# Diff attention: where ScalarE and VectorE do a head's normalisation among the next head's work

## The chip, the cores and the metric

The kernel runs on one core of one Trainium2 chip. The metric is the device time of one execution in microseconds (us); lower is better. The core has five engines that run their own instruction queues in order: TensorE (PE: matrix products and transpositions, written to PSUM banks), VectorE (DVE), ScalarE (ACT), GpSimd (POOL) and SyncE (SP, which here only issues transfers).

## The reference

One decoder layer on 512 tokens of width 1024, in float32. Two attention branches run side by side on the same normalised input; the change lies in the second one, differential attention with four heads:

```python
scores = jnp.einsum('bqhmd,bshmd->bhmqs', qblk, k) * scale      # two maps m per head
scores = scores - slopes[:, None, None, None] * delta           # causal, ALiBi
p = jax.nn.softmax(scores, axis=-1)
a = p[:, :, 0] - lam * p[:, :, 1]
out = jnp.einsum('bhqs,bshe->bqhe', a, v)                       # 128 values per head
...
out = _rmsnorm(out, subln_g) * (1.0 - lam_init)                 # per head and token
...
merged = (sigmoid(ga) * (out_a @ w_branch_swa) + sigmoid(gd) * (out_d @ w_branch_diff))
x = x + gate1 * (merged @ w_out)
```

A gated MLP with a causal convolution and a final RMSNorm follow.

## The kernel before, in words

Every float32 product is done as three products of a high and a low part: `split` makes them, a cast on ScalarE for the high part and a subtraction on VectorE for the low part. TensorE's queue is in an order written out by hand (`manual_schedule`); VectorE, ScalarE and GpSimd are ordered in this stretch by a scheduler that takes what is ready, by priority. `tc.high_priority(offset=HP)` puts a block ahead of other ready work, and `tc.issue_after(x)` keeps what is traced in the block behind instruction `x` on that engine's queue. Every engine then runs its queue strictly in this order, so an instruction that waits holds up all that stand behind it.

TensorE fills the time between the steps of attention with "fillers": each call of `fill(1)` runs one step (three products of 512 columns) of a projection from the list `units`. `after(n, fn)` runs `fn` after n more fillers.

Differential attention goes over 16 blocks, s = 4h + n for head h (0 to 3) and token block n (0 to 3). For each block TensorE makes the scores (`sd`), VectorE adds the distance term and takes the maximum, ScalarE the exponentials, VectorE the difference of the two maps, TensorE turns the result (`td`), and ScalarE and VectorE store it as high and low part (`aTh`, `aTl`). When a head has its four blocks, `diff_values(h)` does:

- TensorE: the products with the values, `od`, in the PSUM bank of tag `v`, of which there is one (`vbank`, bufs=1).
- ScalarE: the square `sq` and the scaled copy `of` of `od`.
- `STAT_LAG[h]` = 6 fillers later, `stats`: TensorE sums the squares (`pss`, the same bank of tag `v`), VectorE makes `ms` from them, GpSimd the inverse root, into four columns of `cols`.
- `ROW_LAG[h]` fillers after that, `to_rows`: TensorE turns the columns (`rs`, again tag `v`), ScalarE copies the piece, GpSimd writes it to DRAM (`rs0d` to `rs3d`) and reads it back as a row on all partitions (`rb`).
- `NORM_LAG[h]` fillers after `stats`, `spread`: VectorE multiplies `of` by `rb`, and `split` writes the high and low part into `vvh` and `vvl`, over the head's values. The product waits in the queue behind the last two weight splits (`recent`).

`of` has two buffers, taken in turn (tags `kvA`, `kvB`); `rb` of heads 0 to 2 has one. `vvh` and `vvl` are read only by the products `pB`, after all heads. Around this stretch VectorE also does modulation rows (`ra`, from `ada_rows`), and both engines split the weights of gates and branches (`wga`, `wba`, `wgd`, `wbd`), which load through four raw buffers that VectorE frees; `ta` and `tdall` are the gates' values.

Of the kernel before, what the change touches and what calls it, by code (L numbers as in the profile page):

```python
# [10 lines left out]
AF = mybir.ActivationFunctionType  # L11
ALU = mybir.AluOpType
# [15 lines left out]
HP = 100000  # L28
# [3 lines left out]
G1_AT = 12  # L32
M5_AT = 4
STAT_LAG = (6, 6, 6, 6)
ROW_LAG = (8, 8, 8, 5)
NORM_LAG = (34, 34, 34, 24)
VA_AT = 5
SWA_FILL = (2, 1, 6, 2, 2, 2, 2, 5, 0)
# [9 lines left out]
def kernel(  # L48
# [19 lines left out]
    nc = tc.nc  # L68
# [25 lines left out]
    def vbank(name, shape=(P, S)):  # L94
        return bank("v", 1, list(shape), name)
# [4 lines left out]
    def to_rows(dst, lo, n, name):  # L100
        turned = vbank(name, (P, P))
        nc.tensor.transpose(turned, cols[:, lo + n - P : lo + n], ident)
        part = cpool.tile([32, P], F32, tag="part", name=name + "p")
        with tc.high_priority(offset=2 * HP):
            nc.scalar.copy(part, turned[96:])
        d = dp.tile([n, P], F32, name=name + "d")
        nc.gpsimd.dma_start(d, part[32 - n :])
        nc.gpsimd.dma_start(dst, d.rearrange("k q -> (k q)").partition_broadcast(P))
# [10 lines left out]
    def split(hi, lo, src):  # L119
        return nc.scalar.copy(hi, src), nc.vector.tensor_sub(lo, src, hi.bitcast(F32))  # L120

    def mm3(o, lh, ll, rh, rl, start, stop):
        nc.tensor.matmul(o, lh, rh, start=start, stop=False)  # L123
        nc.tensor.matmul(o, lh, rl, start=False, stop=False)  # L124
        nc.tensor.matmul(o, ll, rh, start=False, stop=stop)  # L125
# [18 lines left out]
    cv, sublnc = cols[:, 72:160], cols[:, 160:161]  # L144
    sink = cpool.tile([P, 8], F32, name="sink")
    lamv = cpool.tile([P, 4, 64], F32, name="lamv")


    def rstd_start(ssq, n, d, wpool, plus=None):
        ms = wpool.tile([P, n], F32, tag="rs_a", bufs=3, name="ms")  # L150
        if plus is None:
            nc.vector.tensor_scalar(ms, ssq, 1.0 / d, EPS, ALU.mult, ALU.add)
        else:
            nc.vector.scalar_tensor_tensor(ms, ssq, 1.0 / d, plus, ALU.mult, ALU.add)
        r0 = wpool.tile([P, n], F32, tag="rs_c", bufs=3, name="r0")
        nc.gpsimd.tensor_tensor(r0, ms, mhalf[:, :n], ALU.pow)
        return ms, r0
# [24 lines left out]
    def rstd_m2(dst, ssq, n, d, wpool, plus=None):  # L182
        rstd_end(dst, *rstd_start(ssq, n, d, wpool, plus), n, wpool)
# [125 lines left out]
    for p in range(KT // 2):  # L309
        for hf in range(2) if p == 3 else (None,):  # L310
            sl = ALL if hf is None else HALVES[hf]
            sq, xx = (a.rearrange("p (a s) -> p a s", a=2)[:, :, sl] for a in (sqs[p], xT[:, p]))
# [17 lines left out]
    ms = pp.tile([P, NT], F32, tag="rs_a", bufs=3, name="ms")  # L330
# [91 lines left out]
    def evac(hi, lo, src, scale=None):  # L422
        if scale is None:
            nc.scalar.copy(hi, src)
            nc.vector.tensor_sub(lo, src, hi.bitcast(F32))
        else:
            nc.scalar.activation(hi, src, AF.Copy, scale=scale)
            nc.vector.scalar_tensor_tensor(lo, src, scale, hi.bitcast(F32), ALU.mult, ALU.subtract)
# [117 lines left out]
    def after(n, fn):  # L546
        later.append([n, fn])
# [164 lines left out]
    def diff_transpose(s):  # L712
# [7 lines left out]
        with tc.high_priority(offset=HP):  # L720
            evac(hi, lo, tp[:, : (n + 1) * P].rearrange("p (k q) -> p k q", q=P))

    def diff_values(h):
        aTh, aTl = aTs[h]
        o = vbank(f"od{h}")
        for k in range(NT):
            q0 = k * P
            mm3(
                o[:, q0:], vv[0][:, h, k * P : (k + 1) * P], vv[1][:, h, k * P : (k + 1) * P],
                aTh[:, k * AW + q0 : k * AW + 512], aTl[:, k * AW + q0 : k * AW + 512],  # L730
                k == 0, k == NT - 1,
            )
        sq = big.tile([P, S], F32, tag="sq2", name=f"sq{h}")
        of = big.tile([P, S], F32, tag=("kvA", "kvB")[h % 2], name=f"of{h}")
        nc.scalar.activation(sq, o, AF.Square)
        nc.scalar.activation(of, o, AF.Copy, scale=sublnc)

        def stats():
            pss = vbank(f"pss{h}", (P, NT))
            for n in range(NT):  # L740
                nc.tensor.matmul(pss[:, n : n + 1], sq[:, n * P : (n + 1) * P], ones[:, 0:1], start=True, stop=True)
            rs = cols[:, NCOL + NT * h : NCOL + NT * h + NT]
            l0, e0 = sums[h][:, 0], sums[h][:, 1]
            nc.gpsimd.tensor_tensor(e0, l0, l0, ALU.mult)
            nc.gpsimd.tensor_scalar_mul(e0, e0, EPS)
            with tc.high_priority(offset=HP):
                ms, r0 = rstd_start(pss, NT, P, ap, plus=e0)
                t = ap.tile([P, NT], F32, tag="rs_b", bufs=3, name="rt")
                nc.gpsimd.tensor_tensor(t, r0, r0, ALU.mult)
                nc.gpsimd.tensor_tensor(t, t, ms, ALU.mult)  # L750
                nc.gpsimd.tensor_scalar_add(t, t, -3.0)
                nc.gpsimd.tensor_tensor(rs, t, r0, ALU.mult)
            last = h == DIFF_HEADS - 1
            rb = big.tile([P, S], F32, tag="sq2", name="rb3") if last else ap.tile([P, S], F32, tag="rb", name=f"rb{h}")

            def spread():
                with ExitStack() as place:
                    for b in recent:
                        place.enter_context(tc.issue_after(b.ins))
                    nc.vector.tensor_mul(of, of, rb)  # L760
                with tc.high_priority(offset=HP):
                    split(vv[0][:, h], vv[1][:, h], of)

            after(ROW_LAG[h], lambda: to_rows(rb, NCOL + NT * h, NT, f"rs{h}"))
            after(NORM_LAG[h], spread)

        after(STAT_LAG[h], stats)


# [114 lines left out]
    for s in range(4 * DIFF_HEADS):  # L884
        h, n = divmod(s, NT)
        if n == 3 and h < 2:
            waiting = units[:]
            units.clear()
            add_head(h + 2)
            units.extend(waiting)  # L890
        if n == 0 and h:
            for j in ((2,), (3,), (4, 5))[h - 1]:
                add_gate_a(j)
        fill(DIFF_FILL[1])
        nxt = {0: (), 1: (s + 1,), 2: (s + 1,), 3: (s + 1, s + 2)}[n] if s < 15 else ()
        if nxt:
            diff_scores(*nxt)
        fill(DIFF_FILL[2] + (n == 0))
        diff_transpose(s)
        for z in nxt:  # L900
            end = diff_softmax(z)
        if nxt:
            ada_behind(end)
        if n == 0 and h:
            fill(DIFF_FILL[3])
            diff_values(h - 1)
    for j in range(6, KT):
        add_gate_a(j)
    fill(4)
    diff_values(DIFF_HEADS - 1)  # L910
    while units or loaded or current:
        fill(1)
# [341 lines left out]
    ssq, r2, xns = {}, {}, {}  # L1254
# [69 lines left out]
    last = range(KT - TAIL, KT)  # L1324
# [541 lines left out]
```

## Time and profile before

| | |
|---|---|
| runs | 680.58, 680.91, 682.28 us; median 680.91 |
| the profiled execution | 682.48 us, its span 680.7 us |
| mean granted TensorE clock | 0.992 |
| busy share of the span | PE 98%, PEld 87%, DVE 83%, ACT 59%, POOL 12% |
| differential attention and gates, heads 0 to 3 | about 130 to 230 us in the span |

PE is the row of matrix products and PEld that of the weight loads beside them. A row of a timeline gives start, duration, engine, line of the kernel before, operation, output<-input with sizes, and in brackets the idle time just before and what ended it. A row of waits gives who waited for whom: total us, times, longest. A row of windows gives the stretch, its length, each engine's busy time (PE, PEld, DVE, ACT, POOL), the granted clock, the share of the DMA engines and GB/s.

### The profile page before, as it was taken

How to read it: one execution, taken by the hardware profiler on the slowest of the kernel's cores; microseconds unless marked ns; L12 is line 12 of the kernel's file. 1: busy time of each engine (PE TensorE's matmuls, PEld its weight loads, DVE VectorE, ACT ScalarE, POOL GpSimd, SP SyncE). 2: the span in 40 equal slices, each digit the busy share in tenths (PEclk: the TensorE clock that was granted, in tenths of full speed). 3: DMA queues.
4: the chain of work that ended last, by engine and by line, in shares of the span. 5: the costliest groups of instructions: out<-in, count | busy, mean ns of one | idle time of the engine just before them, and what ended most of it. 6: DMA issues, size and time to landing. Idle time of an engine off the chain costs nothing.

```text
span 680.7 us, 10794 instructions
## 1 busy us (share of the span) xinstructions
PE 668.3 (98%) x4021; PEld 593.6 (87%) x4021; DVE 565.0 (83%) x1005; ACT 400.0 (59%) x702; POOL 81.8 (12%) x110
## 2 busy tenths in 40 slices
PE   8999999999998999999999999999999999999995
PEld 7888888888886888888899999999999998888885
DVE  6988987768876559964689998888888999979997
ACT  6678786465744233433497556565556666656665
POOL 2000000012211100010020110011111003440300
PEclk9999999999999899999999999999999999999998
DMA  8961231446355488667473898877976658996903
GB/s 353 408 241 62 94 94 63 140 139 201 98 165 172 141 310 262 230 182 277 130 125 103 212 223 206 187 194 178 216 172 175 150 186 192 194 202 191 165 0 124
DMA packets 71876, 121.78 MB, mean 179 GB/s; under 512 B 4208, under 2 KB 48016, under 8 KB 71824
## 3 DMA queue, kind: packets, MB, share of 16 engines
q1 hardware_dynamic: 52960, 95.04, 41.3%
q0 software_dynamic: 18576, 25.71, 22.1%
q8 instruction: 31, 0.51, 0.3%
q10 hardware_dynamic: 288, 0.34, 0.1%
q14 instruction: 21, 0.17, 0.1%
HBM read 118.97 MB, written 2.11 MB: 178 GB/s over the span
## 4 chain that ended last, share of the span: by engine, by line
PE 66%; DVE 1%; issue 0%; ACT 0%; ACTq 0%
PE up L1192 33%; PE dc L1795 15%; PE pgd L125 2%; PE oc L1249 2%; PE pgd L124 2%; PE oc L1248 2%; PE oc L1252 2%; PE pgd L123 2%; PE pB L125 1%; PE pB L124 1%; PE pB L123 1%; PE th L1288 1%; PE pga L123 0%; PE pga L124 0%; PE pga L125 0%; PE pA L123 0%
## 5 line engine op out<-in xcount | busy, mean ns | idle before, releaser
L1192 PE MATMUL up<-t,m_whi 128*128 128x256 f32 x512 | 93.1, 283 | 0.0
L1192 PEld LDWEIGHTS up<-t,m_whi 128*128 128x128 f32 x512 | 79.9, 192 | 0.0
L1192 PE MATMUL up<-t,m_wlo 128*128 128x256 f32 x256 | 72.4, 283 | 0.0
L1192 PE MATMUL up<-bh,p_whi 128*128 128x256 f32 x232 | 65.7, 283 | 0.0
L1192 PE MATMUL up<-bl,p_whi 128*128 128x256 f32 x232 | 65.7, 283 | 0.0
L1192 PE MATMUL up<-bh,p_wlo 128*128 128x256 f32 x232 | 65.7, 283 | 0.0
L1192 PEld LDWEIGHTS up<-t,m_wlo 128*128 128x128 f32 x256 | 49.2, 192 | 0.0
L1094 POOL DMA_DIRECT2D s<-in_w_up_dram x21 | 27.0, 1362 | 158.2 <-DMA s<-in_w_up_dram 105.5
L1192 PEld LDWEIGHTS up<-bh,p_whi 128*128 128x128 f32 x232 | 44.5, 192 | 0.0
L1192 PEld LDWEIGHTS up<-bl,p_whi 128*128 128x128 f32 x232 | 44.5, 192 | 0.0
L1192 PEld LDWEIGHTS up<-bh,p_wlo 128*128 128x128 f32 x232 | 44.5, 192 | 0.0
L785 DVE CUSTOM_DVE_ANT_0 ra<-ra,csb 128x1024 f32<-128x1024 f32 x32 | 38.7, 1219 | 4.6 <-DMA ra<-in_w_ada_t_dram 4.6
L1122 ACT CAST m_whi<-s 128x1024 fp32r<-128x1024 f32 x31 | 32.5, 1047 | 15.7 <-DVE s L1116 9.1
L1126 DVE TENSOR_TENSOR m_wlo<-s,m_whi 128x1024 fp32r<-128x1024 f32 x31 | 37.8, 1219 | 1.3 <-ACT m_whi L1122 1.3
L1192 PE MATMUL up<-t,p_whi 128*128 128x256 f32 x176 | 32.2, 283 | 0.0
L703 ACT ACTIVATE sd<-sd,dmx 128x128 f32<-128x128 f32 (+3 forms) x32 | 17.7, 555 | 16.8 <-DVE dmx L688 16.6
L1192 PEld LDWEIGHTS up<-t,p_whi 128*128 128x128 f32 x176 | 27.4, 192 | 0.1
L1122 ACT CAST p_whi<-wa 128x1024 fp32r<-128x1024 f32 x18 | 18.8, 1043 | 12.6 <-PE up L1192 7.2
L1199 ACT ACTIVATE gT<-a,cols 128x512 f32<-128x512 f32 x22 | 17.6, 813 | 13.3 <-DVE a L1234 13.0
L1126 DVE TENSOR_TENSOR p_wlo<-wa,p_whi 128x1024 fp32r<-128x1024 f32 x18 | 22.0, 1222 | 4.0 <-ACT p_whi L1122 3.2
L1192 PE MATMUL up<-t,p_wlo 128*128 128x256 f32 x88 | 24.9, 283 | 0.0
L1116 DVE TENSOR_TENSOR s<-s,wa 128x1024 f32<-128x1024 f32 x20 | 24.4, 1219 | 0.1
(550 smaller groups left out, 2040.4 us busy)
## 6 DMA issues: line engine op xcount, KB each, us to landing
ra<-in_w_ada_t_dram SPq DMA_DIRECT2D x32, 512.0 KB, 4.1
wa<-in_w_up_dram SPq DMA_DIRECT2D x22, 512.0 KB, 4.1
s<-in_w_up_dram SPq DMA_DIRECT2D x21, 512.0 KB, 4.4
s<-in_w_up_dram POOLq DMA_DIRECT2D x21, 512.0 KB, 6.6
adaw<-in_w_ada_t_dram SPq DMA_DIRECT2D x15, 512.0 KB, 10.2
a<-in_w_up_dram SPq DMA_DIRECT2D x11, 512.0 KB, 4.7
b<-in_w_down_dram SPq DMA_DIRECT2D x10, 512.0 KB, 4.0
w<-in_w_first_dram SPq DMA_DIRECT2D x8, 512.0 KB, 10.2
```

What stands on the lines that cost most here:

```text
L123: nc.tensor.matmul(o, lh, rh, start=start, stop=False)
L124: nc.tensor.matmul(o, lh, rl, start=False, stop=False)
L125: nc.tensor.matmul(o, ll, rh, start=False, stop=stop)
L703: nc.scalar.activation(pm[m], pm[m], AF.Exp, bias=mx[:, m : m + 1], scale=-1.0, accum_out=(l0, l1)[m])
L785: nc.vector.tensor_tensor_reduce(r, r, csb, 1.0, 0.0, ALU.mult, ALU.add, late_mod[:, idx : idx + 1])
L1094: nc.gpsimd.dma_start(dst, upblock(*blk), accum_op=ALU.add)
L1116: nc.vector.tensor_add(src, src, R[J, "a11" if name == "m6" else "a12"])
L1122: nc.scalar.copy(W[J, name][0], R[J, SRC[name]])
L1126: nc.vector.tensor_sub(lo, R[J, SRC[name]], hi.bitcast(F32))
L1192: nc.tensor.matmul(o[u], w[:, k, cu], b[:, k], start=name in ("p1", "m5", "p2") and k == 0 and x == 0, stop=k == 3 and x == 2, skip_group_ ...
L1199: nc.scalar.activation(grow(j), av[J][:, u], AF.Identity, bias=cv[:, 66 + j : 67 + j], scale=cv[:, 44 + j : 45 + j])
L1795: nc.tensor.matmul((bank2[u] if o is None else o)[:, sl], a[:, q, cu], b[:, q, sl], start=first_mm and x == 0, stop=last_mm and x == 2, sk ...
```

## The change

Four edits:

1. In `diff_values`, the square and the copy of `od` on ScalarE get high priority.
2. In `spread`, for heads 0 to 2, the product of head h on VectorE is kept behind `ms` of head h+1 (`summed`).
3. There too, the split is kept behind the copy `of` of head h+1 on ScalarE (`emptied`).
4. `ROW_LAG` of head 2 is 6 in place of 8: its roots are turned two fillers sooner.

```diff
-ROW_LAG = (8, 8, 8, 5)
+ROW_LAG = (8, 8, 6, 5)
...
+    root_in = [None]
+
     def rstd_start(ssq, n, d, wpool, plus=None):
...
-            nc.vector.scalar_tensor_tensor(ms, ssq, 1.0 / d, plus, ALU.mult, ALU.add)
+            root_in[0] = nc.vector.scalar_tensor_tensor(ms, ssq, 1.0 / d, plus, ALU.mult, ALU.add)
...
+    emptied, summed = {}, {}
+
     def diff_values(h):
...
-        nc.scalar.activation(sq, o, AF.Square)
-        nc.scalar.activation(of, o, AF.Copy, scale=sublnc)
+        with tc.high_priority(offset=HP):
+            nc.scalar.activation(sq, o, AF.Square)
+            emptied[h] = nc.scalar.activation(of, o, AF.Copy, scale=sublnc)
...
                 ms, r0 = rstd_start(pss, NT, P, ap, plus=e0)
+                summed[h] = root_in[0]
...
                     for b in recent:
                         place.enter_context(tc.issue_after(b.ins))
+                    if not last:
+                        place.enter_context(tc.issue_after(summed[h + 1].ins))
                     nc.vector.tensor_mul(of, of, rb)
-                with tc.high_priority(offset=HP):
+                with tc.high_priority(offset=HP), ExitStack() as place:
+                    if not last:
+                        place.enter_context(tc.issue_after(emptied[h + 1].ins))
                     split(vv[0][:, h], vv[1][:, h], of)
```

The names of the built order carry the head: `of2` is the scaled copy of head 2, `pss3` the sums of head 3. The line numbers of the changed kernel are a few higher. First place: ScalarE's queue where head 3's result is copied out of its bank. Before:

```order
L424 CAST aTh3_2015<-td3_3_2172 128x4x128
L735 ACTIVATE sq3_2224<-od3_2211 128x512
L120 CAST vvh_582<-of2_2043 128x512
L736 ACTIVATE of3_2225<-od3_2211,cols_82 128x512
L120 CAST wgd0_h_2346<-wgd0_2344 128x1024
L796 ACTIVATE ta_1225<-pga6_2198 128x512
L120 CAST wbd0_2358<-wbd0_2356 128x1024
```

The same stretch of ScalarE's queue now:

```order
L426 CAST aTh3_2015<-td3_3_2172 128x4x128
L740 ACTIVATE sq3_2224<-od3_2211 128x512
L741 ACTIVATE of3_2225<-od3_2211,cols_82 128x512
L120 CAST wgd0_h_2346<-wgd0_2344 128x1024
L806 ACTIVATE ta_1225<-pga6_2198 128x512
L120 CAST vvh_582<-of2_2043 128x512
L120 CAST wbd0_2358<-wbd0_2356 128x1024
```

The cast of head 2's split (`vvh<-of2`) stood between head 3's square and copy; it now stands behind the copy, a weight cast and a gate. Second place: VectorE's queue in the same stretch, around the two last modulation rows and `ms` of head 3. Before:

```order
L785 ISA ra15_2321,late_mod_624<-ra15_2321,csb_189 128x1024
L785 ISA late_mod_624 128x1
L760 TENSOR_TENSOR of2_2043<-of2_2043,rb2_2093 128x512
L120 TENSOR_TENSOR vvl_583<-of2_2043,vvh_582 128x512
L120 TENSOR_TENSOR wgd0_l_2347<-wgd0_2344,wgd0_h_2346 128x1024
L154 SCALAR_TENSOR_TENSOR ms_2255<-pss3_2248,dls3_1960 128x4
L813 SCALAR_TENSOR_TENSOR ta_1225<-ta_1225,pA6_2241 128x512
L120 TENSOR_TENSOR wbd0_2358<-wbd0_2356,wbd0_2358 128x1024
L120 TENSOR_TENSOR wgd1_l_2353<-wgd1_2350,wgd1_h_2352 128x1024
```

The same stretch of VectorE's queue now:

```order
L795 ISA ra15_2321,late_mod_624<-ra15_2321,csb_189 128x1024
L795 ISA late_mod_624 128x1
L120 TENSOR_TENSOR wgd0_l_2347<-wgd0_2344,wgd0_h_2346 128x1024
L156 SCALAR_TENSOR_TENSOR ms_2255<-pss3_2248,dls3_1960 128x4
L768 TENSOR_TENSOR of2_2043<-of2_2043,rb2_2093 128x512
L823 SCALAR_TENSOR_TENSOR ta_1225<-ta_1225,pA6_2241 128x512
L120 TENSOR_TENSOR vvl_583<-of2_2043,vvh_582 128x512
L120 TENSOR_TENSOR wbd0_2358<-wbd0_2356,wbd0_2358 128x1024
L120 TENSOR_TENSOR wgd1_l_2353<-wgd1_2350,wgd1_h_2352 128x1024
```

Head 2's product moved from ahead of the weight split `wgd0_l` and of `ms` (the row that reads `pss3`) to behind both, and its low part to behind the gate update `ta`. Third place: VectorE's queue earlier, at the scores of head 3's last block (`sd3_3`). Before:

```order
L154 SCALAR_TENSOR_TENSOR ms_2084<-pss2_2077,dls2_1724 128x4
L425 TENSOR_TENSOR aTl3_2016<-td3_1_2094,aTh3_2015 128x2x128
L688 ISA sd3_3_0_2120,dmx3_3_2119<-sd3_3_0_2113,ddf_167 128x512
L688 ISA dmx3_3_2119 128x1
L688 ISA sd3_3_1_2122,dmx3_3_2119<-sd3_3_1_2114,ddf_167 128x512
L688 ISA dmx3_3_2119 128x1
L706 RECIPROCAL dls3_1960<-dls3_1960 128x1
L707 SCALAR_TENSOR_TENSOR dls3_1960<-dls3_1960,nlam_699 128x1
L708 SCALAR_TENSOR_TENSOR sd3_3_0_2120<-sd3_3_1_2122,dls3_1960,sd3_3_0_2120 128x512
```

The same stretch now, with head 1's two rows in it:

```order
L156 SCALAR_TENSOR_TENSOR ms_2084<-pss2_2077,dls2_1724 128x4
L427 TENSOR_TENSOR aTl3_2016<-td3_1_2094,aTh3_2015 128x2x128
L768 TENSOR_TENSOR of1_1796<-of1_1796,rb1_1851 128x512
L690 ISA sd3_3_0_2120,dmx3_3_2119<-sd3_3_0_2113,ddf_167 128x512
L690 ISA dmx3_3_2119 128x1
L690 ISA sd3_3_1_2122,dmx3_3_2119<-sd3_3_1_2114,ddf_167 128x512
L690 ISA dmx3_3_2119 128x1
L120 TENSOR_TENSOR vvl_583<-of1_1796,vvh_582 128x512
L708 RECIPROCAL dls3_1960<-dls3_1960 128x1
L709 SCALAR_TENSOR_TENSOR dls3_1960<-dls3_1960,nlam_699 128x1
L710 SCALAR_TENSOR_TENSOR sd3_3_0_2120<-sd3_3_1_2122,dls3_1960,sd3_3_0_2120 128x512
```

Head 1's product and its low part (`vvl<-of1`) now stand among these rows; they stood before the scores of the block before. Head 0's moved in the same way to the scores of head 2's last block. On TensorE only `rs2` moved: from two fillers behind the transposition `td3_2` to just ahead of it.

## The prediction

> **What bounds the kernel now.** I read the page first, then TensorE's own waits, then the windows around its one long wait, then what ScalarE and VectorE did there.
>
> ```profile
> span 680.7 us, 10794 instructions
> PE 668.3 (98%) x4021; PEld 593.6 (87%) x4021; DVE 565.0 (83%) x1005; ACT 400.0 (59%) x702; POOL 81.8 (12%) x110
> ```
> ```profile
> PE pss L741 <- ACT of L736: 2.8, 1, 2.8
> PE ava L234 <- POOL ones L131: 1.1, 1, 1.1
> ```
>
> TensorE is the bound, so only its idle time and its clock can be won. In the whole middle of the program it waits once: the sums `pss` of head 3 wait for ScalarE's copy `of` (L736). The windows (us; busy time of PE, PEld, DVE, ACT, POOL; granted clock; DMA) show that the wait has a second price:
>
> ```profile
> 216.60:219.56 2.96, 0.17 (x2) 0.01 (x1) 1.31 (x2) 1.26 (x3) 0.00 (x0) 0.97 0.42 169
> 219.56:221.28 1.72, 1.72 (x8) 1.72 (x9) 0.89 (x2) 1.72 (x3) 0.00 (x0) 0.50 0.00 0
> 223.00:226.00 3.00, 3.00 (x8) 2.32 (x8) 1.70 (x2) 0.00 (x0) 0.82 (x4) 0.50 0.39 147
> 227.00:230.00 3.00, 3.00 (x16) 2.40 (x15) 0.00 (x0) 0.26 (x1) 0.62 (x1) 1.00 0.55 176
> ```
>
> After the wait the granted clock is 0.50, and it is back at 1.00 only by 227. Why `of` was late stands in ScalarE's and VectorE's timelines (start, duration, work, idle before it):
>
> ```profile
> 212.70 0.60 ACT L735 ACTIVATE sq<-od 128x512 f32<-128x512 f32 x1 [3.82 <-PE od L125]
> 218.30 0.62 ACT L120 CAST vvh<-of 128x512 fp32r<-128x512 f32 x1 [5.00 <-DVE of L760]
> 218.82 0.68 ACT L736 ACTIVATE of<-od,cols 128x512 f32<-128x512 f32 x1
> ```
> ```profile
> 217.57 0.69 DVE L760 TENSOR_TENSOR of<-of,rb 128x512 f32<-128x512 f32 x1 [4.64 <-DMA rb<-rs2d]
> 221.61 0.15 DVE L154 SCALAR_TENSOR_TENSOR ms<-pss,dls 128x4 f32<-128x4 f32 x1
> ```
>
> Between the square of head 3 and its copy, ScalarE's queue holds the cast `vvh` of head 2. That cast waits for VectorE's product `of2*rb2`, which waits 4.64 us for the row `rb2` to land. So head 3's copy, whose input `od3` was there at 212.7, ends at 219.5. `pss3` shares the one bank of tag v with `od3` and starts behind the copy; `ms3`, the first step of head 3's roots, runs at 221.61.
>
> **The change part by part.** *Head 3's copy goes ahead of head 2's cast.* The stall's price comes from TensorE's starts:
>
> ```profile
> 212.73 0.40 PE L124 MATMUL pga<-hTlA,wga_h 128*128 128x512 f32 x1
> 216.37 0.39 PE L125 MATMUL pA<-outah,wba_l 128*128 128x512 f32 x1
> 219.56 1.86 PE L741 MATMUL pss<-ones,sq 128*128 128x1 f32 x8 [2.79 <-ACT of L736]
> 221.28 0.77 PE L123 MATMUL pA<-outah,wba_h 128*128 128x512 f32 x1
> 226.40 0.40 PE L123 MATMUL pga<-hThA,wga_h 128*128 128x512 f32 x1
> 198.60 0.95 PE L741 MATMUL pss<-ones,sq 128*128 128x1 f32 x8
> 199.40 0.41 PE L718 MATMUL td<-ident,sd 128*128 128x128 f32 x2
> ```
>
> The first two starts are 16 products apart: 3.64/16 = 0.2275 us each. The product at 216.37 is thus done with at 216.60, and the wait is 219.56 - 216.60 = 2.96. `pss3` takes 221.28 - 219.56 = 1.72 to the next start, head 2's took 199.40 - 198.60 = 0.80: 0.92 lost. From 221.28 to 226.40 stand 12 products: 5.12, against 12 x 0.2275 = 2.73: 2.39 lost. Sum: **2.96 + 0.92 + 2.39 = 6.27 us**. With nothing ahead of it, `of3` would follow `sq3` at about 213.3 and end by 214; TensorE asks for the bank at 216.6, so the whole term goes, with 2.6 us to spare.
>
> [...]
>
> *What is late next on TensorE.* Head 2's product now stands on VectorE behind `ms3`, which needs `pss3`. Behind the product stand the `ta` update, the split's low part, and two weight splits. I cost this at nothing: `rb2` landed at 217.57, and `ms3` can now be read at about 216.60 + 0.95 = 217.6. Without that cover VectorE would hold these splits, but gate weights are ready far ahead of use, as the sixth of them shows (low part, then its first product):
>
> ```profile
> 258.89 1.23 DVE L120 TENSOR_TENSOR wgd_l<-wgd,wgd_h 128x1024 fp32r<-128x1024 f32 x1
> 271.61 0.39 PE L123 MATMUL pgd<-hThA,wgd_h 128*128 128x512 f32 x1
> ```
>
> That is 271.6 - 260.1 = 11.5 us, more than the 6.27 by which TensorE would come sooner. The transfers of that stretch are issued as VectorE frees raw buffers, so they move along.
>
> *Head 1's product and split move too*, and this is a loss. They stood in a stretch where VectorE then idled; now the product stands between `ms2` and the scores of head 3's last block, and the low part behind those scores.
>
> ```profile
> 201.61 0.16 DVE L154 SCALAR_TENSOR_TENSOR ms<-pss,dls 128x4 f32<-128x4 f32 x1
> 202.02 0.68 DVE L688 CUSTOM_DVE_ANT_0 sd<-sd,ddf 128x512 f32<-128x512 f32 x1
> 204.36 0.17 DVE L706 RECIPROCAL dls<-dls 128x1 f32<-128x1 f32 x1 [1.04 <-ACT sd L703]
> 209.96 0.68 DVE L425 TENSOR_TENSOR aTl<-td,aTh 128x512 fp32r<-128x512 f32 x1
> 210.56 1.21 DVE L785 CUSTOM_DVE_ANT_0 ra<-ra,csb 128x1024 f32<-128x1024 f32 x1
> ```
> ```profile
> 202.80 0.72 ACT L703 ACTIVATE sd<-sd,dmx 128x512 f32<-128x512 f32 x1 [2.58 <-DVE dmx L688]
> 203.53 0.71 ACT L703 ACTIVATE sd<-sd,dmx 128x512 f32<-128x512 f32 x1
> ```
> ```profile
> PEld od L124 <- DVE aTl L425: 0.3, 1, 0.3
> ```
>
> The last `aTl` of head 3 already ends (210.64) where TensorE wants it for `od3`; a weight load waited 0.3 us for it. A row of 512 columns moves VectorE on by 0.60 us (209.96 to 210.56). With the product at 202.02, the scores start at 202.62 and the first of them ends at 203.30. ScalarE casts `vvh` meanwhile: from 202.71, and it moves on by 0.52 (218.30 to 218.82), to 203.23. So the first exponential starts at about 203.33 in place of 202.80, and the reciprocal 0.53 later, at 204.89. The low part (203.92 to 204.52) fits in ahead of it, in the idle time. So `aTl` comes 0.53 us later, and TensorE with it. Bounds: 0 (VectorE's earlier stretch, now empty, brings `ms2` forward; TensorE gains nothing from an `aTl` that is early) and 1.20 (both rows exposed). I take **0.6**, near the worked value; the little on top is for head 2's stretch, where two weight splits change places with a modulation row and with head 3's first probabilities, so that `ms2` may be late.
>
> *Head 0's product and split* move likewise to the scores of head 2; TensorE turns that block late enough:
>
> ```profile
> 180.97 0.75 DVE L708 SCALAR_TENSOR_TENSOR sd<-sd,dls,sd 128x512 f32<-128x512 f32 x1
> 185.14 0.60 PE L718 MATMUL td<-ident,sd 128*128 128x128 f32 x4
> ```
>
> Both rows and a 0.5 us `aTl` ahead of the first still leave about 1.5 us. Cost nothing.
>
> *Head 2's roots are turned two fillers sooner.* TensorE's transposition moves from 206.45 to just ahead of the `td` at 204.73; the roots it reads are ready on POOL by 204.07:
>
> ```profile
> 203.87 0.20 POOL L752 TENSOR_TENSOR cols<-rt,r 128x4 f32<-128x4 f32 x1
> 205.71 1.05 POOL L744 TENSOR_TENSOR dls<-dls 128x4 f32<-128x4 f32 x1 [1.64 <-DVE sd L708]
> 207.32 0.60 POOL L107 DMA_DIRECT2D rs2d<-rs2p  x1 [0.25 <-ACT rs2p L105]
> ```
> ```profile
> 204.73 0.49 PE L718 MATMUL td<-ident,sd 128*128 128x128 f32 x3
> 206.45 0.27 PE L102 MATMUL rs<-ident,cols 128*128 128x128 f32 x1
> ```
>
> Spare: 0.66 us, so no wait expected (0 to 0.5). The row does not land sooner: POOL's L744 stands ahead of the write, waits for head 3's last probabilities (0.5 us later now), and then takes 1.05. `rb2` lands at 217.6 to 218.1. *Head 3's roots* lose the slow clock that covered them: 15 products after `pss3` is 216.60 + 0.80 + 3.41 = 220.8; `ms3` at 217.6 plus POOL's 2.46 (201.61 to 204.07) is 220.1. Spare 0.7; cost 0, at most 0.5.
>
> Sum against the profiled execution's 682.48 (span 680.70 and 1.78 around it): 682.48 - 6.27 + 0.6 = **676.8 us**. The runs timed are 680.58, 680.91 and 682.28: two groups, some 1.5 apart, and the profiled one in the upper. Half of the cold loss (3.31/2 = 1.66) would explain that, if the lower runs ran cold half as long. Then the median gives 680.91 - 2.96 - 1.66 + 0.6 = 676.9, the same.
>
> **The rivals.** *More is won* (chance 0.10). If the median lost the full 6.27 too, and `aTl` costs nothing to 0.6, it is 674.6 to 675.2. For it: nothing shows the other runs' clocks. Against: the two groups.
>
> *The new wait cools TensorE again* (0.08). An idle 0.6 at `od3`, perhaps with one at the roots, costs half or all of 3.31: 678.5 to 680.1. Against: the 1.1 us wait of the start, behind which the granted clock stayed at 1.00:
>
> ```profile
> 0.00:3.40 3.40, 2.27 (x10) 2.28 (x11) 0.06 (x1) 1.49 (x2) 2.32 (x18) 1.00 0.37 112
> ```
>
> *Slower* (0.06). The place is `od3`: every late microsecond on VectorE reaches TensorE there. If the wait w is long enough to cool it, the cost is w + 3.31, and it decides at w = 2.96; at 3.5 it is 676.2 + 6.8 = 683.0. That takes a row `rb1` that lands after 204, ahead of head 3's scores. It was used at 191.63 before:
>
> ```profile
> 191.63 0.69 DVE L760 TENSOR_TENSOR of<-of,rb 128x512 f32<-128x512 f32 x1 [0.33 <-DMA rb<-rs1d]
> ```
>
> *Nothing changes* (0.06): the copy does move, as the built order shows, but TensorE comes 6 us sooner to the gates and waits for gate or output weights instead: 680.9. Against: the 11.5 us above.
>
> **How the numbers follow.** Forecast 0.70. 0.3% is 2.04 us, about what a measurement here can tell from no change, so faster means under 678.87. Faster: 0.70 + 0.10 + half of the second rival = 0.84. Same: its other half and the last rival = 0.10. Slower: 0.06. The range, 675.0 to 679.0, takes in most of the first rival, the bounds of 0 to 1.2 at `od3`, 0.5 at the roots, and the cheaper half of the second.
>
> **What would show it.** Right: `of` directly behind `sq` at about 213, no wait at `pss3`, the clock at 1.00 throughout 216 to 230, a wait of half a microsecond at `od3` for `aTl`, `rb2` landing no sooner. Wrong: a clock of 0.50 anywhere in 205 to 230, a wait at either transposition of roots over 0.5, or waits of TensorE on gate weights after 225.

## The result, and the profile after

| | before | after |
|---|---|---|
| runs, median | 680.91 us (680.58 to 682.28) | 677.43 us (677.24 to 678.63, 5 runs) |
| the profiled execution, its span | 682.48, 680.7 us | 677.43, 675.4 us |
| mean granted TensorE clock | 0.992 | 0.997 |
| from the start of `pss2` to the first gate product `pgd` | 34.77 us | 29.56 us |

The ratio is 0.9952 [0.9937, 0.9966]: faster, by more than the 0.3% that can be told here. The forecast was 676.8 in 675.0 to 679.0.

The profile after begins with TensorE's own waits (who waited for whom: total, times, longest). The wait at `pss` is gone, and a new one stands at `rs`, the turning of head 3's roots:

```profile
span 675.4 us, 10792 instructions
PE rs L102 <- POOL cols L758: 0.6, 1, 0.6
```

The windows (us; busy time of PE, PEld, DVE, ACT, POOL; granted clock; DMA share; GB/s) show the stretch that ran at a granted clock of 0.50 before:

```profile
216.00:218.00 2.00, 2.00 (x15) 1.79 (x14) 1.37 (x3) 0.95 (x2) 0.00 (x0) 1.00 0.93 326
218.00:220.00 2.00, 2.00 (x10) 1.62 (x9) 1.26 (x4) 1.35 (x2) 1.74 (x3) 1.00 0.73 263
220.00:223.00 3.00, 2.41 (x12) 1.69 (x11) 1.79 (x3) 0.48 (x2) 1.80 (x4) 1.00 0.23 75
223.00:226.00 3.00, 3.00 (x15) 2.48 (x14) 0.00 (x0) 0.49 (x1) 0.68 (x2) 1.00 0.46 163
```

The clock is 1.00 throughout, and the only idle time, 0.59 us, lies in 220 to 223. ScalarE's timeline shows why the bank was free in time: head 3's copy follows its square directly, and the cast of head 2's split comes 5 us behind it.

```profile
212.90 0.60 ACT L740 ACTIVATE sq<-od 128x512 f32<-128x512 f32 x1 [4.09 <-PE od L125]
213.39 0.69 ACT L741 ACTIVATE of<-od,cols 128x512 f32<-128x512 f32 x1
218.65 0.62 ACT L120 CAST vvh<-of 128x512 fp32r<-128x512 f32 x1 [1.70 <-DVE of L768]
```

TensorE's starts give the stretch in its steps: `pss2`, the first product of `od3` that reads `aTl`, `pss3`, `rs3`, `pgd` (rows between them are left out):

```profile
198.66 0.94 PE L746 MATMUL pss<-ones,sq 128*128 128x1 f32 x8
210.89 0.50 PE L124 MATMUL od<-aTl,vvh 128*128 128x512 f32 x1
216.80 0.95 PE L746 MATMUL pss<-ones,sq 128*128 128x1 f32 x8
221.90 0.33 PE L102 MATMUL rs<-ident,cols 128*128 128x128 f32 x1 [0.59 <-POOL cols L758]
228.22 0.39 PE L123 MATMUL pgd<-hThA,wgd_h 128*128 128x512 f32 x1
```

Before, the last of these stood at:

```profile
233.37 0.39 PE L123 MATMUL pgd<-hThA,wgd_h 128*128 128x512 f32 x1
```

`pss2` started at 198.60 before and 198.66 after, so nothing changed ahead of this stretch; from `pgd` to the span's end it is 447.3 us before (680.7 - 233.37) and 447.2 after. The whole gain lies between: `pss3` starts 2.76 us sooner (219.56 to 216.80), and the way from there to `pgd` is 13.81 before and 11.42 after.

The new wait is read from GpSimd and VectorE side by side, from head 3's `ms` on:

```profile
218.11 1.42 POOL L158 TENSOR_TENSOR r<-ms,mhalf 128x4 f32<-128x4 f32 x1 [5.62 <-DVE ms L156]
219.60 0.20 POOL L755 TENSOR_TENSOR rt<-r 128x4 f32<-128x4 f32 x1
219.88 0.20 POOL L756 TENSOR_TENSOR rt<-rt,ms 128x4 f32<-128x4 f32 x1
220.18 0.56 POOL L757 TENSOR_SCALAR rt<-rt 128x4 f32<-128x4 f32 x1
220.82 1.02 POOL L758 TENSOR_TENSOR cols<-rt,r 128x4 f32<-128x4 f32 x1
```
```profile
217.86 0.16 DVE L156 SCALAR_TENSOR_TENSOR ms<-pss,dls 128x4 f32<-128x4 f32 x1
217.94 0.68 DVE L768 TENSOR_TENSOR of<-of,rb 128x512 f32<-128x512 f32 x1
219.36 0.69 DVE L823 SCALAR_TENSOR_TENSOR ta<-ta,pA 128x512 f32<-128x512 f32 x1 [0.74 <-ACT vvh L120]
219.96 0.68 DVE L120 TENSOR_TENSOR vvl<-of,vvh 128x512 fp32r<-128x512 f32 x1
220.57 1.22 DVE L120 TENSOR_TENSOR wbd<-wbd,wbd 128x1024 fp32r<-128x1024 f32 x1
```

The same five steps are 1.05, 0.19, 0.20, 0.24 and 0.20 before, and take 2.22 from start to end (221.85 to 224.07); here it is 3.73 (218.11 to 221.84). The last two of before:

```profile
223.55 0.24 POOL L751 TENSOR_SCALAR rt<-rt 128x4 f32<-128x4 f32 x1
223.87 0.20 POOL L752 TENSOR_TENSOR cols<-rt,r 128x4 f32<-128x4 f32 x1
```

Three of them are lengthened in the changed kernel, and two end just as a VectorE row does whose two inputs both lie in SBUF: L757 at 220.74, `vvl` at 220.64; L758 at 221.84, `wbd` at 221.79. The two steps beside `ta`, which reads one input from PSUM (`pA`), keep their 0.20.

### The profile page after: what moved, and what is told of

Same layout as the page of the kernel before. It is cut to its first block, busy times and chain, and to the rows that moved or that the text cites. A ratio compares the mean times of both kernels' runs of the same rounds, so it can differ in the third digit from the quotient of the medians.

```text
span 675.4 us, 10792 instructions
## 1 busy us (share of the span) xinstructions
PE 665.7 (99%) x4021; PEld 591.5 (88%) x4021; DVE 564.3 (84%) x1005; ACT 400.1 (59%) x702; POOL 84.9 (13%) x110
## 4 chain that ended last, share of the span: by engine, by line
PE 97%; DVE 1%; DMA 1%; POOL 1%; ACT 0%; issue 0%; DVEq 0%; ACTq 0%
PE up L1202 33%; PE dc L1805 15%; PE av L368 3%; PE pgd L123 2%; PE oc L1258 2%; PE pgd L124 2%; PE oc L1262 2%; PE oc L1259 2%; PE pgd L125 2%; PE pga L123 2%; PE pga L125 2%; PE pga L124 2%; PE aqa L365 2%; PE sd L679 2%; PE sw L581 1%; PE pk L123 1%
```

## The experiments

Times are medians; ratios are to the kernel before on the same chip. "The stretch" is from the start of `pss2` to the first `pgd` in the profiled execution. In all 13 profiled executions the rest of the span is 645.8 to 646.2 us, so the stretch holds all that differs between them.

**e1: the priority alone.** The kernel before, with the square and the copy of `od` at high priority and no ties:

```diff
-        nc.scalar.activation(sq, o, AF.Square)
-        nc.scalar.activation(of, o, AF.Copy, scale=sublnc)
+        with tc.high_priority(offset=HP):
+            nc.scalar.activation(sq, o, AF.Square)
+            nc.scalar.activation(of, o, AF.Copy, scale=sublnc)
```

> The kernel before, with the high priority on the square and the copy of od and nothing else. In the built order one row moves: the copy of3 goes ahead of the cast vvh of head 2 on ScalarE. Theory: the wait at pss3 goes, but ms3 still stands on VectorE behind head 2's product (which waits for rb2 until 217.6), its low part and a weight split, so ms3 runs at about 220.8 and the roots are ready at about 223.3, while TensorE wants them at 220.8: a wait of about 2.5 us at the transposition of head 3's roots. If that wait cools TensorE again, most of the gain is lost (679 to 681 us); if it does not, 677.5 to 679. Rival: the copy was all that held TensorE up, and this alone gives what the whole change gave, 677.2 to 677.6.

Measured: 679.19 (678.16 to 680.14), ratio 0.9964 [0.9947, 0.9981]; stretch 30.38. `pss3` starts at 216.60 and the clock is 1.00. The prediction put it at 216.60 without the stall; that the hundredths agree is chance, since `pss2` starts 0.12 later in this execution (17.88 after `pss2`, against 18.00). But head 2's product, low part and a weight split stay ahead of `ms3` on VectorE, and the roots' wait is twice that of the changed kernel:

```profile
216.60 0.95 PE L742 MATMUL pss<-ones,sq 128*128 128x1 f32 x8
222.78 0.33 PE L102 MATMUL rs<-ident,cols 128*128 128x128 f32 x1 [1.18 <-POOL cols L753]
```

That is 1.18 and not the 2.5 that was expected, and part of it is luck: the row `rb2` landed 1.14 us sooner in this execution than in that of before (217.57), so head 2's product was out of the way sooner, and `ms3` started at 219.90 and not at 220.8.

```profile
216.43 0.69 DVE L761 TENSOR_TENSOR of<-of,rb 128x512 f32<-128x512 f32 x1 [3.67 <-DMA rb<-rs2d]
```

So the order of two instructions on ScalarE's queue takes the stall and the cold stretch away; what the ties add is to free VectorE's queue ahead of `ms3`. That this is worth something is read from the traces: the intervals of this ratio and of the whole change's overlap.

**e2: the ties alone.** The changed kernel without the priority, and `ROW_LAG` as before:

```diff
-ROW_LAG = (8, 8, 6, 5)
+ROW_LAG = (8, 8, 8, 5)
...
-        with tc.high_priority(offset=HP):
-            nc.scalar.activation(sq, o, AF.Square)
-            emptied[h] = nc.scalar.activation(of, o, AF.Copy, scale=sublnc)
+        nc.scalar.activation(sq, o, AF.Square)
+        emptied[h] = nc.scalar.activation(of, o, AF.Copy, scale=sublnc)
```

> The changed kernel without the high priority and with ROW_LAG of head 2 back at 8: only the two ties are left. In the built order ScalarE and VectorE stand as in the changed kernel, but for the copy of head 2's turned roots. Theory: the same time as the changed kernel within 0.3 us (677.2 to 677.7), since the row rb2 landed no sooner there. Rival: the two fillers sooner are needed for rb2, and head 2's product is late without them; then 1 to 2 us above the changed kernel.

Measured: 677.92 (676.71 to 678.70), ratio 0.9940 [0.9923, 0.9957]; stretch 29.85, clock 1.00, the same 0.59 at the roots. The ties put the copy ahead by themselves; beside them the priority and the sooner turning add nothing that can be measured.

**e3: the sooner turning alone.** The kernel before with:

```diff
-ROW_LAG = (8, 8, 8, 5)
+ROW_LAG = (8, 8, 6, 5)
```

> The kernel before with ROW_LAG of head 2 at 6 in place of 8 and nothing else. Theory: rb2 lands 0.1 to 0.4 us sooner, because GpSimd's two small steps for head 3 stand ahead of the write, so the wait at pss3 shrinks from 2.8 to 2.4 to 2.7 and the time falls by no more than 0.5 us. Rival: rb2 lands two fillers, about 1.7 us, sooner; the wait is 1.1 and TensorE does not cool, 4 to 5 us less.

Measured: 681.90 (679.42 to 683.42), ratio 0.9994 [0.9980, 1.0008]; stretch 34.60. `pss3` still waits 2.73 us, from 216.7 to 219.43, and the clock is 0.50 behind it. Head 2's product starts at 217.44, 0.13 sooner than before: the turning alone is worth nothing.

**e4: the stall kept, the clock held up.** The kernel before, with 13 small products without use on TensorE ahead of `pss3`, so that it has something to do while it waits:

```diff
+            if h == DIFF_HEADS - 1:
+                busy = sbank("busy", (P, P))
+                for _ in range(WARM):
+                    nc.tensor.matmul(busy, ones, ones, start=True, stop=True)
```

> The kernel before with 13 small products of ones by ones, into a free bank, ahead of pss3, some 2.6 us of work that fits in TensorE's wait. Nothing else changes and the wait of the copy stays. Theory: the granted clock stays at 1.00 through 216 to 230, and what is won is the cold loss alone: 3.3 us against a run that ran cold as long as the profiled one, half of it (1.7) against one that ran cold half as long. pss3 still starts at about 219.6. Rival: the clock has nothing to do with the idle time, and the time stays at that of before or grows.

Measured: 680.38 (679.19 to 681.51), ratio 0.9977 [0.9965, 0.9989]; stretch 32.20. `pss3` starts about as late as before (219.33 against 219.56), and the clock is never reduced (windows as above):

```profile
216.60:219.33 2.73, 2.73 (x27) 2.73 (x27) 1.39 (x2) 1.70 (x3) 0.00 (x0) 1.00 0.58 228
219.33:222.00 2.67, 2.67 (x18) 2.37 (x17) 1.42 (x3) 1.88 (x3) 0.81 (x1) 1.00 0.00 0
```
```profile
219.33 0.95 PE L746 MATMUL pss<-ones,sq 128*128 128x1 f32 x8
224.42 0.33 PE L103 MATMUL rs<-ident,cols 128*128 128x128 f32 x1 [0.61 <-POOL cols L757]
```

The two prices come apart: the useful work is held up as long as before, and the cold stretch behind it is not there. In this execution the copy itself was done by 218.84 (`rb2` landed sooner here too, and head 2's product started at 216.91), and it is the added products that last until 219.33. That they, and not a shorter wait, keep the clock up rests on the runs: all 11 have a mean granted clock of 0.997 to 0.999, where 38 of 45 runs of the kernel before have 0.992 to 0.995. The roots' wait appears here too, at a clock of 1.00 and with VectorE's old order, beside a weight split: one of GpSimd's steps takes 1.16 there (222.59 to 223.75, the split 222.48 to 223.70), where before it took 0.20. So it comes with the full clock and does not need the ties.

**e5: head 3's roots turned two fillers later.** The changed kernel with:

```diff
-ROW_LAG = (8, 8, 6, 5)
+ROW_LAG = (8, 8, 6, 7)
```

> The changed kernel with ROW_LAG of head 3 at 7 in place of 5: its roots are turned two fillers, 1.4 us, later. Theory: the roots were 0.6 us late at the transposition in the changed kernel, so the wait goes and the time falls by 0.6 to 0.9 us below the changed kernel (676.4 to 676.8); rb3 lands a microsecond later, which nobody waits for before the products pB. Rival: the wait is only moved to another place (the product of head 3 or the first pB), and the time is that of the changed kernel.

Measured: 676.88 (676.40 to 678.06), ratio 0.9943 [0.9926, 0.9959]; stretch 28.44. GpSimd's five steps take 3.74 as in the changed kernel, but nobody waits for them:

```profile
216.57 0.95 PE L746 MATMUL pss<-ones,sq 128*128 128x1 f32 x8
222.29 0.27 PE L102 MATMUL rs<-ident,cols 128*128 128x128 f32 x1
227.18 0.39 PE L123 MATMUL pgd<-hThA,wgd_h 128*128 128x512 f32 x1
```

From `pss3` to `pgd` it is 10.61 against 11.42: the roots' wait of 0.59 costs **0.81 us**. With this, 10.61 is the same work without any wait, so the cold stretch of before cost 13.81 - 10.61 = **3.20** (predicted 0.92 + 2.39 = 3.31). e4 won less than that, 2.57 in the stretch, because the roots' wait came in its place.

**e6 and e7: what lengthens GpSimd's steps.** Two rows without use are put on VectorE among those behind `ms3`, writing 512 columns where nothing is read any more. In e6 both inputs lie in SBUF, in e7 the one input lies in PSUM:

```diff
+                    mul = nc.vector.tensor_mul(of, of, rb)
+                if h == 2:
+                    with tc.high_priority(offset=2 * HP), tc.issue_after(mul.ins):
+                        for _ in range(2):
+                            nc.vector.tensor_tensor(heads[2][:, 0], csb[:, :S], csb[:, S:], ALU.add)   # e6
+                            nc.vector.tensor_copy(heads[2][:, 0], turned_last[0])                      # e7
```

> The changed kernel with two more rows of 512 columns on VectorE around head 2's product, while GpSimd makes head 3's roots; each adds two operands that lie in SBUF, into a tile that nobody reads any more. Theory: a VectorE row with two SBUF operands holds up GpSimd's small steps for as long as it runs, so the roots come later than in the changed kernel (3.98 us from ms3 to the end of cols there): 4.0 to 4.7, and the wait at the transposition is 0.6 to 1.3. Rival: GpSimd's steps are slow by themselves at this place, and the wait stays at 0.6 whatever VectorE does.

> The same with two rows of 512 columns that copy from PSUM in place of the two that add from SBUF: the same length on VectorE, no two SBUF operands. Theory: these do not hold GpSimd up, and they push the split's low part and the next weight split behind the roots, so the roots come sooner than in the changed kernel, 2.6 to 3.4 us after ms3, the wait at the transposition is 0 to 0.2, and the kernel is up to 0.6 us faster than the changed one in spite of the added work. Rivals: VectorE being busy at all is what holds GpSimd up, then it is as slow as with the rows from SBUF; or GpSimd is slow by itself, then the wait stays at 0.6.

Measured: e6 677.05 (676.35 to 677.93), ratio 0.9942 [0.9927, 0.9956], stretch 28.75; e7 676.91 (676.02 to 677.58), ratio 0.9937 [0.9922, 0.9952], stretch 29.00. e7's rows on GpSimd and VectorE:

```profile
218.33 1.42 POOL L158 TENSOR_TENSOR r<-ms,mhalf 128x4 f32<-128x4 f32 x1 [5.53 <-DVE ms L156]
...
220.40 0.23 POOL L758 TENSOR_SCALAR rt<-rt 128x4 f32<-128x4 f32 x1
220.72 0.20 POOL L759 TENSOR_TENSOR cols<-rt,r 128x4 f32<-128x4 f32 x1
```
```profile
220.18 0.68 DVE L773 CAST qk<-td 128x512 fp32r<-128x512 f32 x1
220.78 0.68 DVE L120 TENSOR_TENSOR vvl<-of,vvh 128x512 fp32r<-128x512 f32 x1
```

Beside the row that reads PSUM, L758 and L759 keep 0.23 and 0.20, where the changed kernel had 0.56 and 1.02; the five steps take 2.59, and TensorE no longer waits at the roots: from `pss3` to `pgd` it is 10.61, as in e5. In e6, with a row of two SBUF inputs in the same place (219.58 to 220.26) and `vvl` behind it (220.18 to 220.87), they are lengthened again, and each ends within 0.1 us of the row that it overlaps:

```profile
219.79 0.56 POOL L758 TENSOR_SCALAR rt<-rt 128x4 f32<-128x4 f32 x1
220.44 0.49 POOL L759 TENSOR_TENSOR cols<-rt,r 128x4 f32<-128x4 f32 x1
```
```profile
219.58 0.68 DVE L773 TENSOR_TENSOR qk<-csb 128x512 fp32r<-128x512 f32 x1
220.18 0.69 DVE L120 TENSOR_TENSOR vvl<-of,vvh 128x512 fp32r<-128x512 f32 x1
```

e6 was meant to make the roots later than in the changed kernel, and did not: the chain there is 3.21 (3.46 from `ms3`, where 4.0 to 4.7 was expected), and from `pss3` to `pgd` it is 10.89. e6 has the shorter stretch of the two even so, because `od3` came later in e7's execution (below). Its rows push `wbd`, the longest, to 221.38, behind the chain, so the last step stands beside a row of 0.69 instead of one of 1.22. In these traces a step behind `r` that started inside a row of two SBUF inputs took what was left of that row and 0.05 to 0.10 more: e6's last had 0.43 of `vvl` left and took 0.49, the changed kernel's had 0.97 of `wbd` left and took 1.02. The number of such rows did not decide it: e6's L758 ended at 220.35, though the next of them had started at 220.18.

**f1 to f4: on one chip.** f1 is the changed kernel again, f2 is e5 again. f3 is f2 with `ROW_LAG = (8, 8, 8, 7)`. f4 is f2 with the ties of head 2 alone:

```diff
-                    if not last:
+                    if h == DIFF_HEADS - 2:
                         place.enter_context(tc.issue_after(summed[h + 1].ins))
...
-                    if not last:
+                    if h == DIFF_HEADS - 2:
                         place.enter_context(tc.issue_after(emptied[h + 1].ins))
```

> The changed kernel once more, as the base for the three below on one chip. Theory (the stall and its cold stretch are gone, and TensorE waits 0.6 us for head 3's roots in their place): from the start of pss2 to the first product of the gates pgd 29.4 to 29.9 us (29.56 in the first profile; 34.77 before the change), rs3 waits 0.6 us, median 677.2 to 677.9. If its profile falls among its longer runs (span about 676.5), the place of the 1.2 us between its two groups of runs is read from it.

> The changed kernel with head 3's roots turned two fillers later, beside the changed kernel on one chip. Theory (the roots' wait cost 0.8 with its restart): pss2 to pgd 28.4 to 28.8, no wait at rs3, median 0.6 to 1.0 below the changed kernel's. Rival (the wait is hidden, since what follows is late too): the same median within 0.3.

> As the one with head 3's roots two fillers later, but head 2's roots are turned where they were before the change. Theory (the row's write stands behind another step of GpSimd in either case, so turning it sooner wins nothing): the same as with it, pss2 to pgd 28.4 to 28.8, median within 0.3. Rival (the row lands later, and head 2's product with it, and VectorE holds the splits behind it): 0.3 to 1.0 longer.

> As the one with head 3's roots two fillers later, but only head 2's product and split are tied; those of heads 0 and 1 go back to where they stood before the change, ahead of the scores. Theory (head 1's two rows among the scores of head 3's last block are what made od3 wait): the product od3 starts within 0.1 us of its turn whatever VectorE's position, so pss2 to pgd is 28.3 to 28.5, and the median is 0 to 0.3 below. Rival (the wait at od3 comes from where VectorE stands in the execution, not from head 1's rows): od3 waits 0 to 0.3 as in the other kernels.

| | median (lowest to highest) | ratio | stretch | span |
|---|---|---|---|---|
| f1 | 677.50 (677.25 to 678.15) | 0.9948 [0.9933, 0.9963] | 29.34 | 675.4 |
| f2 | 677.36 (676.44 to 678.27) | 0.9945 [0.9930, 0.9961] | 28.45 | 674.4 |
| f3 | 676.85 (676.82 to 677.54) | 0.9938 [0.9924, 0.9953] | 28.85 | 674.8 |
| f4 | 676.89 (676.46 to 677.27) | 0.9936 [0.9921, 0.9951] | 29.26 | 675.5 |

The traces of f1 and f2 repeat the 0.9 us between them, but the medians lie only 0.14 apart, with runs of f2 spread over 1.8 us. f2's trace is also no proof of the later turning: GpSimd's five steps take 2.60 there, in the same kernel in which they took 3.74 in e5. Its product started 0.25 after `ms3` (217.59) and not 0.08, about when `rb2` landed, so that `r` started with it and not inside it:

```profile
217.84 0.73 DVE L768 TENSOR_TENSOR of<-of,rb 128x512 f32<-128x512 f32 x1
217.84 1.04 POOL L158 TENSOR_TENSOR r<-ms,mhalf 128x4 f32<-128x4 f32 x1 [5.46 <-DVE ms L156]
```

Its roots were ready at 220.44, and the changed kernel turns them 4.51 after `pss3` (216.53 in f2), at 221.04: they would have been in time there too. That the later turning takes the wait away is shown where the steps took 3.73 or 3.74 and `pss3` to `pgd` was 10.61 to 10.63 even so: in the traces of e5, f3 and f4, and not in the times. f3 confirms that the sooner turning of head 2's roots gives nothing; the 0.40 that its stretch is longer than f2's lies ahead of `pss3`, where `od3` came later. No version stands clear of the changed kernel's interval.

f4 contradicts the theory that it was sent with. Without head 1's rows among the scores, `od3` waited longer, not less: 0.39 us. VectorE came late to that block, since its weight split waited for ScalarE's cast, and that for the weight itself. f4's rows:

```profile
196.22 1.05 ACT L120 CAST wga_h<-wga 128x1024 fp32r<-128x1024 f32 x1 [2.43 <-DMA wga<-in_w_tiles_dram]
202.57 0.15 DVE L156 SCALAR_TENSOR_TENSOR ms<-pss,dls 128x4 f32<-128x4 f32 x1
211.66 0.50 PE L124 MATMUL od<-aTl,vvh 128*128 128x512 f32 x1 [0.39 <-DVE aTl L427]
```

The same cast in the changed kernel, and in e3, whose order on VectorE is that of before:

```profile
194.91 1.05 ACT L120 CAST wga_h<-wga 128x1024 fp32r<-128x1024 f32 x1 [2.87 <-DMA wga<-in_w_tiles_dram]
```
```profile
193.66 1.05 ACT L120 CAST wga_h<-wga 128x1024 fp32r<-128x1024 f32 x1 [0.46 <-DMA wga<-in_w_tiles_dram]
```

The load was issued at 190.1 to 190.5 in all 13 profiled executions, and `ms2` starts 6.29 to 6.36 us after this cast in every one, so it is the landing that moves it. Set against `pss2`, the starts of `ms2` and of the first product of `od3` that reads `aTl` then fall on two lines (us after the start of `pss2`):

| head 1's rows | `ms2`, then `od3` |
|---|---|
| ahead of the scores | e1 1.26, 12.08; e3 1.32, 12.07; e4 2.50, 12.09; before 3.01, 12.10; f4 3.66, 12.75 |
| among the scores | e5 1.97, 12.06; e6 2.12, 12.06; f2 2.26, 12.06; f1 2.36, 12.07; after 2.55, 12.23; f3 2.64, 12.33; e7 2.80, 12.49; e2 2.85, 12.53 |

With TensorE's turn at 12.06, `od3` is late by what `ms2` exceeds 2.38 when head 1's rows stand among the scores (after: 2.55 - 2.38 = 0.17, measured 0.17), and by what it exceeds 2.97 when they don't (f4: 3.66 - 2.97 = 0.69, measured 0.69). Theory and rival were both half right: the tie takes 2.97 - 2.38 = 0.59 us of slack, and the landing of one weight decides how much of that is paid. (The way from `ms2` to the reciprocal of head 3's last block gives the same 0.59: 2.75 before, 3.34 after.)

## Why the prediction was right, point by point

**The stall and the cold clock: right.** Predicted 6.27; the runs show 2.96 for the stall (from `pss2` to `pss3` it is 20.96 before and 17.88 in e1, which is 3.08, but 0.12 of that lies at `od3`, where TensorE waited a little before too) and 3.20 for the clock (e5), together 6.16. e4 separates the two and e1 shows that the copy's place is enough for both.

**The two groups of runs: there, but not by half.** The prediction had no clock for the runs and took it that the lower ones ran cold half as long (1.66). Beside the experiments the kernel before ran 45 times: 19 runs with a mean granted clock of 0.992 or 0.993 and a median span of 681.0, 19 with 0.994 or 0.995 and 679.0, and 7 with 0.998 or 0.999 and 678.4. So there are three groups. The last lies 2.6 below the first, about what e4 won with the clock held up (2.57), and its clock is e4's (0.997 to 0.999): by that it did not cool. The second lies 2.0 below the first: near the 1.66, but most of those 2.6 and not half. No run shows the 1.66, a stretch cooled for half as long; what the runs show in its place are these differences of 2.0 and 2.6. Nor is it shown why one stall costs more in one run than in another: the stall itself may have been shorter in those runs, for head 2's product, whose cast held the copy up, started between 216.43 (e1) and 217.57 (before) in the four traces with the old order on VectorE, and the only two traces of an uncovered stall, before and e3, are both of the first group. Whatever the cause, the runs differ, and so the median gained less (3.48) than the profiled execution (5.05), which belongs to the first group. That the kernels without the stall still spread over 0.7 to 2.0 us, at clocks of 0.995 to 0.999, is not explained.

**`od3`'s wait: the size of the tie right, the term mis-sized.** The step "the reciprocal 0.53 later ... so `aTl` comes 0.53 us later, and TensorE with it" is 0.59 in slack, but took it that the slack was used up whole. `od3` came only 0.13 later after `pss2` than before (12.23 against 12.10), since `ms2` ran 0.46 sooner. The bound of 0 named this, with the wrong reason: it is not the emptied stretch of VectorE that moves `ms2` but the landing of the weight `wga`, whose cast starts at 193.6 to 196.2 over these executions. That the cost was as small as this is partly luck of the profiled execution: in e2, with the same order on VectorE, `od3` stood at 12.53. The wait of half a microsecond that was to show the prediction right was 0.17.

**Head 3's roots: wrong.** "`ms3` at 217.6 plus POOL's 2.46 ... is 220.1. Spare 0.7; cost 0, at most 0.5" failed in the 2.46. It was taken from head 2's roots in the trace of before, where VectorE ran other rows beside them. From the start of `ms3` to the end of `cols` it took 217.86 to 221.84, 3.98, and cost 0.81, above the bound; the wait of 0.59 meets one of the prediction's own signs of being wrong (over 0.5 at a transposition of roots). The rows that the change itself moved behind `ms3` (`of2*rb2`, `vvl`) are among those beside which the steps were longer: 1.42 for 1.05 and 0.56 for 0.24. The trace of before had such a row, which the prediction did not use: at head 1's roots GpSimd's 0.20 step took 1.28, beside a weight split. Another stands in the prediction itself, L744 at 205.71: it took 1.05 beside a modulation row, and 0.20 at 181.88 without one.

```profile
179.20 1.28 POOL L750 TENSOR_TENSOR rt<-rt,ms 128x4 f32<-128x4 f32 x1
179.20 1.22 DVE L120 TENSOR_TENSOR wga_l<-wga,wga_h 128x1024 fp32r<-128x1024 f32 x1
```

**Head 2's roots: right.** No wait, and the row no sooner: its write was issued at 207.32 before and after, behind GpSimd's step on the probabilities (f3 and e3: worth nothing), and `rb2` landed at about 217.8 (issued at 211.92, 5.9 us to landing), within the 217.6 to 218.1 that was predicted.

```profile
207.32 0.61 POOL L107 DMA_DIRECT2D rs2d<-rs2p  x1
```

**Weights for the gates: right.** No wait of TensorE on gate weights stands among its waits, though it reached them 5.2 us sooner.

**The sum.** In the profiled executions: -6.16 (stall, clock) + 0.13 (`od3`) + 0.81 (roots) = -5.22; measured in the stretch 29.56 - 34.77 = -5.21, in the span -5.3. The execution around the span is 0.25 longer (2.03 against 1.78); the prediction held it constant. It is 1.95 to 2.08 in after, e2, e5, f1, f2 and f3, and 1.72 to 1.87 in the others, e6, e7 and f4 with ties among them; why is open. So the forecast of 676.8 missed the profiled 677.43 by 0.63: 0.81 too little at the roots, 0.25 around the span, 0.11 too much at the clock, less 0.47 too much at `od3` and 0.09 in the rest of the span (0.61, the rest is rounding).

**The rivals.** Nothing cooled TensorE again: waits of 0.59 and 1.18 (e1) left the clock at 1.00 in the profiled executions. One of e1's seven runs has a mean clock of 0.995 and is about 1 us longer than their median; whether a longer wait for the roots cooled it, as was feared for e1, no trace shows. The median did not lose the full 6.27, TensorE did not wait long at `od3`, and the gates did not wait for weights, so the other three rivals did not come about either.

## What to carry to other kernels

Look for an instruction that frees a shared buffer and stands in an in-order queue behind one that waits for something else, here a cast that waited for a row from DRAM: moving it adds no work, and the stall of 2.96 us on TensorE cost 6.16 here. When a stall goes, everything that it covered is due earlier, so give the steps behind it, here two fillers, their old lead again. Price a chain of small steps by the rows that will run beside it in the new order, not by its time elsewhere in the program, and give it a range: the same five steps took 3.74 and 2.60 in two executions of one kernel.

## What the runs showed of the hardware

GpSimd's small steps were longer beside VectorE's rows of two SBUF inputs: a step on four columns that takes 0.19 to 0.25 without such a row took 0.46 to 1.28 when it started inside one (0.49 in e6, 1.28 in before), and ended 0.05 to 0.10 us after it; beside a row that reads PSUM it took 0.20 to 0.23 (e6, e7). What in the hardware does this no run shows. The other way it is not seen in the traces' times: in e1 GpSimd's `r` ran from 220.14 to 221.18, and a VectorE split of two SBUF inputs started inside it and took its usual 1.22 (in f2, where both started at 217.84, VectorE's row took 0.73 in place of 0.68):

```profile
220.14 1.04 POOL L156 TENSOR_TENSOR r<-ms,mhalf 128x4 f32<-128x4 f32 x1 [9.03 <-DVE ms L154]
221.27 0.57 POOL L750 TENSOR_TENSOR rt<-r 128x4 f32<-128x4 f32 x1
```
```profile
220.57 1.22 DVE L120 TENSOR_TENSOR wbd<-wbd,wbd 128x1024 fp32r<-128x1024 f32 x1
```

The step behind it, L750, took 0.57 and ended at 221.84, the split at 221.79. Why `r` took 1.42 in place of 1.04 where it started inside `of2*rb2`, though it ended well behind it, is open. And behind idle times of 2.79 us (before) and 2.73 us (e3) TensorE's granted clock was 0.50; behind those of 0.59 (after) and 1.18 (e1) it stayed at 1.00. Of 45 runs of the kernel before, 38 have a mean granted clock of 0.992 to 0.995, and the other 7 one of 0.998 or 0.999, as without a cold stretch (e4: 0.997 to 0.999).
